# A two-layer decoder trunk on one core: gate columns moved into the value projection, feed-forward loads two units ahead, linear-attention outputs grouped by rows, first loads reordered, half of the compression copies on GpSimd

## The chip, the cores and the metric

The kernel runs on one core of a Trainium2 chip. The metric is the device time of one execution in microseconds (us), the median over runs. The core has five engines with an instruction queue each: TensorE (PE, matmuls), VectorE (DVE), ScalarE (ACT), GpSimd (POOL) and SyncE (SP, which only issues DMA transfers). An engine runs its queue in order; an instruction that waits for another engine or a transfer holds up all that stand behind it.

## What is computed

A trunk of two layers on x of 1024 tokens by 1024 channels, in fp32. The first mixes with gated linear attention and with cross-attention to a memory of 256 tokens; the second with native sparse attention (NSA) and the same kind of memory attention. Each is followed by a convolutional feed-forward network.

```
# layer A
q, k, v, r, alr, mq = split_cols(h @ w_in, [GLA_QK, GLA_QK, GLA_V, GLA_V, GLA_RANK, MEM_WIDTH])
...
# linear attention, chunk by chunk, with the state S
o_inter = jnp.einsum('bthd,bhde->bhte', qc * jnp.exp(b), S)
o = o_inter + jnp.einsum('bhts,bhse->bhte', attn, vc)
...
# after layer A, once: six key and value tensors
kv = (rmsnorm(x, g_kv) @ w_kv).reshape(B, T, 6, NSA_GROUPS, NSA_DH)
k_c, v_c, k_s, v_s, k_w, v_w = [kv[:, :, i] for i in range(6)]
...
# compressed blocks: 16 + 16 tokens each, plus a position term, through a small MLP
blocks = jnp.concatenate([sub[:, i:i + ncmp] for i in range(n_sub)], axis=2)
blocks = blocks + pe[:, None, :]
```

Layer B projects the normalised x to 512 NSA queries, 24 branch gates (three for each of eight heads, through a sigmoid) and 512 memory queries.

## The kernel before

The tokens are worked in two halves of 512. A tile holds 128 channels (or 128 tokens) on the partitions. A value that goes through PE at full precision is split in a high part (ACT, fp32r) and a low part (DVE, the difference), and a projection is three matmuls per 128 channels: high by high, high by low, low by high (`projg`, lines 192 to 194). `wraw` loads 128x1024 weights over SP, `wsplit` splits them (lines 176 and 177). The names with r and l at their end (wqkr, wqkl) are such parts. The program records all instructions first and a scheduler orders them on each engine by their dependences; `follow` pins one instruction behind another, and `weave` and `blend` interleave two streams of work by given weights. Buffers are rings: `U` 14 tiles of 128x512, `V` 32 of 128x1024, raw weights 4, split weights 6.

The start (`mix_a`, `stats`, `qkv_a`): x comes in eight tiles over SP, the first weights behind the first of them, the constants over ACT and POOL. ACT squares x for the norm, splits the weights and makes the high parts h (line 227), DVE the low parts (line 228); then four qk projections follow, the results scaled by the norm afterwards.

Linear attention (`gla`): a chunk's outputs go are, for each of four heads, a matmul from the state (line 835: 64 rows, since two heads share a tile) and one from the masked products A with the values (line 842: 128 rows). Both are plain fp32, which PE runs as a pair of instructions each. The four heads are done one after another; the first chunk has no state.

Feed-forward (`Up`, `run`): 22 units, each with two raw tiles wu (four loads over SP), splits into A, Ah and Al (ACT line 978, DVE line 979), sums of weight columns on POOL, and matmuls into fx, fy and fw (lines 1014 to 1016). The raw tiles and the split tiles have rings of two units. `run` works one unit and prepares the next: it issues the next unit's loads at its own beginning.

Before layer B (`mix_b`): for each half and for kind 0 and 1 (compressed keys and values), `front` projects to kc, scales it by the norm rs to kcs (DVE line 1450), and `comp_in` copies it into the block layout ck: eight copies per kind and half, on ACT (lines 1458 and 1459), with a step of 16 elements in the source. When both halves are in, DVE adds the position term pe (line 1465), and the matmuls hid read ck. `front` then projects the gates from a packed 24-column weight (`packed`, lines 219 and 220: a 128x512 matmul for 24 columns in use) to gsb, which matmuls gateT (line 1549) turn to token rows: ope. `MemKV(1)` projects the memory's keys mk meanwhile, from the split weights wmkr and wmkl. `values` projects the sparse attention's values nv: 256 columns for each 128 tokens (lines 1618 to 1620), with the weights wnv scaled by the norm's gain on DVE or POOL.

## Time and profile before

| | us |
|---|---|
| median of three runs | 2321.58 |
| lowest and highest | 2311.52, 2324.42 |
| the profiled execution | 2315.45 |
| its span | 2313.7 |
| PE busy | 2256.4 (98%) |
| DVE busy | 1735.4 (75%) |
| ACT busy | 1139.0 (49%) |
| POOL busy | 365.4 (16%) |

The profile is of one execution. The span runs from its first to its last instruction. A share of busy time is a mean over stages that differ; what an engine waits for is in the views of waits and the timeline, and the clock that TensorE was granted is in the windows: 1.00 is 2.4 GHz, and there are two levels, 2.4 and 1.2 GHz.

### The profile page before, as it was taken

The numbers are of one execution on the slowest core, as the hardware profiler recorded it, in microseconds if no ns is written. First come the engines' busy times: TensorE is split into PE (matmuls) and PEld (weight loads), VectorE is DVE, ScalarE is ACT, GpSimd is POOL, SyncE is SP. The second block draws the span as 40 slices with busy tenths as digits, with TensorE's granted clock in tenths as the row PEclk, the third lists the DMA queues.
The fourth block names the chain that finished last, engine by engine and source line by source line (L and its number), as shares of the span: only waits on it lengthen the run. The fifth ranks groups of instructions, "written<-read, shape, count | busy, mean of one in ns | idle before, by whom it ended". The sixth has DMA issues, their size and how long they took to land.

```text
span 2313.7 us, 31260 instructions
## 1 busy us (share of the span) xinstructions
PE 2256.4 (98%) x11062; PEld 1839.1 (79%) x11062; DVE 1735.4 (75%) x3086; ACT 1139.0 (49%) x2081; POOL 365.4 (16%) x333
## 2 busy tenths in 40 slices
PE   8999999999999999999999999999999999999998
PEld 6888777877788888888888877767887888888886
DVE  6785776887876768886656688885888777667877
ACT  5463544543333334456544588774543343334445
POOL 1211310004322210000002121110003422210000
PEclk9999999999999999999999999999999999999999
DMA  6333236433433329543421111007434433228533
GB/s 212 101 108 95 64 130 210 139 112 135 137 105 113 100 81 340 176 132 125 128 74 53 41 39 45 8 22 240 148 129 137 141 105 110 96 83 323 183 98 110
DMA packets 138893, 284.96 MB, mean 123 GB/s; under 512 B 16086, under 2 KB 22403, under 8 KB 138736
## 3 DMA queue, kind: packets, MB, share of 16 engines
q1 hardware_dynamic: 130144, 262.20, 34.7%
q0 software_dynamic: 3840, 12.24, 1.6%
q10 hardware_dynamic: 4752, 8.51, 1.0%
q8 instruction: 87, 1.43, 0.3%
q14 instruction: 70, 0.57, 0.1%
HBM read 211.06 MB, written 71.83 MB: 122 GB/s over the span
## 4 chain that ended last, share of the span: by engine, by line
PE 84%; DVE 7%; DMA 4%; ACT 3%; issue 2%; SPq 1%; POOL 0%; DVEq 0%; ACTq 0%; POOLq 0%
PE dn L1342 5%; PE dn L1341 5%; PE dn L1343 5%; PE fy L1014 5%; PE fy L1016 4%; PE fy L1015 4%; PE fx L1014 3%; PE no L1753 3%; PE fx L1015 3%; PE fx L1016 3%; PE fw L1016 3%; PE fw L1015 3%; PE fw L1014 3%; PE npt L1737 2%; PE op L193 2%; PE op L192 2%
## 5 line engine op out<-in xcount | busy, mean ns | idle before, releaser
L1342 PE MATMUL dn<-db,da 128*128 128x512 f32 (+1 forms) x628 | 242.4, 386 | 0.8 <-DVE db L1271 0.6
L1341 PE MATMUL dn<-db,da 128*128 128x512 f32 (+1 forms) x628 | 242.5, 386 | 0.0
L1343 PE MATMUL dn<-db,da 128*128 128x512 f32 (+1 forms) x628 | 241.7, 385 | 0.0
L1014 PE MATMUL fy<-B,Ah 128*128 128x512 f32 x496 | 195.1, 393 | 11.3 <-DVE q L1048 6.6
L1016 PE MATMUL fy<-B,Al 128*128 128x512 f32 x496 | 193.6, 390 | 0.4 <-DVE Al L979 0.4
L1015 PE MATMUL fy<-B,Ah 128*128 128x512 f32 x496 | 193.5, 390 | 0.0
L978 ACT ACTIVATE Ah<-wu 128x1024 fp32r<-128x1024 f32 x124 | 130.4, 1052 | 100.9 <-PE fy L1015 60.3
L998 POOL TENSOR_TENSOR wu<-wu,wu 128x512 f32<-128x512 f32 x36 | 49.3, 1369 | 744.4 <-DVE Al L979 410.6
L979 DVE TENSOR_TENSOR Al<-wu,Ah 128x1024 fp32r<-128x1024 f32 x124 | 158.0, 1275 | 6.6 <-ACT Ah L978 6.6
L1342 PEld LDWEIGHTS dn<-db,da 128*128 128x128 f32 x628 | 117.9, 188 | 26.4 <-DVE db L1271 2.6
L1016 PE MATMUL fw<-B,Al 128*128 128x512 f32 x352 | 137.8, 391 | 0.0
L1341 PEld LDWEIGHTS dn<-db,da 128*128 128x128 f32 x628 | 118.0, 188 | 24.3 <-issue 0.2
L1015 PE MATMUL fw<-B,Ah 128*128 128x512 f32 x352 | 137.1, 389 | 0.0
L1014 PE MATMUL fw<-B,Ah 128*128 128x512 f32 x352 | 137.0, 389 | 0.0
L1343 PEld LDWEIGHTS dn<-db,da 128*128 128x128 f32 x628 | 117.9, 188 | 23.3
L1271 DVE TENSOR_TENSOR db<-bl,db 128x512 fp32r<-128x512 f32 x154 | 105.6, 686 | 27.2 <-ACT db L1270 26.6
L1014 PEld LDWEIGHTS fy<-B,Ah 128*128 128x128 f32 x496 | 93.4, 188 | 36.3 <-DVE q L1048 10.4
L1270 ACT ACTIVATE db<-bl 128x512 fp32r<-128x512 f32 x154 | 95.7, 621 | 30.2 <-PE dn L1343 20.8
L1016 PEld LDWEIGHTS fy<-B,Al 128*128 128x128 f32 x496 | 93.4, 188 | 20.7 <-DVE Al L979 1.1
L1015 PEld LDWEIGHTS fy<-B,Ah 128*128 128x128 f32 x496 | 93.4, 188 | 18.9
L192 PE MATMUL op<-om,wor 128*128 128x512 f32 x256 | 103.1, 404 | 2.2 <-ACT om L224 2.2
L1270 ACT ACTIVATE da<-wb 128x512 fp32r<-128x512 f32 x88 | 55.0, 629 | 101.9 <-PE dn L1342 64.6
(427 smaller groups left out, 6176.4 us busy)
## 6 DMA issues: line engine op xcount, KB each, us to landing
wu<-in_w_up_dram SPq DMA_DIRECT2D x176, 256.0 KB, 3.1
bl<-gb_d SPq DMA_DIRECT2D x154, 256.0 KB, 2.7
gb_d<-fc SPq DMA_DIRECT2D x132, 256.0 KB, 3.0
wb<-in_w_down_dram SPq DMA_DIRECT2D x44, 256.0 KB, 4.5
wa<-in_w_down_dram SPq DMA_DIRECT2D x22, 512.0 KB, 7.8
wo<-in_a_wo_dram SPq DMA_DIRECT2D x16, 512.0 KB, 3.7
xre<-om_d SPq DMA_DIRECT2D x32, 256.0 KB, 4.7
x_r<-x SPq DMA_DIRECT2D x32, 256.0 KB, 2.6
```

What stands on the lines that cost most here:

```text
L192: mm(ps, wr[:, k, :], hr, start=(k == 0), stop=False)
L978: a = nc.scalar.activation(hi, src, AF.Copy)
L979: b = nc.vector.tensor_tensor(lo, src, f(hi), ALU.subtract)
L1014: mm(ps, wr, hr, start=(first and j == 0), stop=False, skip_group_check=True)
L1015: mm(ps, wr, hl, start=False, stop=False, skip_group_check=True)
L1016: mm(ps, wl, hr, start=False, stop=(stop and j == 3), skip_group_check=True)
L1270: nc.scalar.activation(w[:, hs(0)], t, AF.Copy)
L1271: b = tt(w[:, hs(1)], t, f(w)[:, hs(0)], ALU.subtract)
L1341: mm(o, hi, bh, start=first, stop=False, skip_group_check=True)
L1342: mm(o, hi, bl, start=False, stop=False, skip_group_check=True)
L1343: mm(o, lo, bh, start=False, stop=stop or n == NP - 1, skip_group_check=True)
L1753: mm(acc[a * 64 : a * 64 + 64, :256], v, pf[:, a * 256 : (a + 1) * 256], start=(n == 0), stop=(n == last[a]),)
```

## The change

Five edits.

1. First loads. The first weights come in two halves, each behind one of the first two tiles of x; the gains that h needs come as a small tile cg of their own over ACT's queue; the other constants (cs, idu, wal, mskf) go over SP behind the second weights. ACT makes all h before any square (the squares are pinned behind, `Norm.past`); a projection's result is scaled once rs is there. Fourteen 128x128 fp32 matmuls on a constant tile are put at PE's beginning.

2. Linear attention: the matmuls of a chunk are ordered by their rows, 128-row ones of two heads, then the four from the state, then the other two of 128 rows.

3. Feed-forward: `run` gets the unit after next, and issues its loads (`ahead`) behind the split of the third and fifth parts.

4. Compression: of each pair of copies the second goes to POOL.

5. Gates: the 24 gate columns stand behind the 256 value columns, so nv has 280 columns, token rows already; `values` scales both parts by their gains, and makes ope from the last 24 columns. The packed weight, its projection, gsb, fold and gateT go.

```diff
+    warm = PS("warm")
+    for _ in range(14):
+        mm(warm[:, :P], on_d, on_d, start=True, stop=True)
...
             for k2 in range(4):
                 t = V(s="x0")
                 tv = t.rearrange("p (k t) -> p k t", k=2)
                 if half == 0:
                     for i in range(2):
-                        last_x[0] = nc.sync.dma_start(tv[:, i, :], x[2 * k2 + i, :, hs(half)])
-                        if k2 + i == 0:
-                            w0.append(wraw(a_w[2], s="wqk"))
+                        nc.sync.dma_start(tv[:, i, :], x[2 * k2 + i, :, hs(half)])
+                        if k2 == 0:
+                            nc.sync.dma_start(raw[:, hs(i)], a_w[2, :, hs(i)])
...
-                        h.append(rl(tv[:, i, :], col(C_MIX + 2 * k2 + i), s="h"))
-                        if k2 + i == 0:
-                            w0[0] = wsplit(w0[0], s="wqk")
+                        k = 2 * k2 + i
+                        t = V(F32R, "h")
+                        h.append((t[:, :HT], t[:, HT:]))
+                        if k2 == 0:
+                            rl_into(wr[:, hs(i)], wl[:, hs(i)], raw[:, hs(i)])
+                        n.past = rl_into(*h[-1], tv[:, i, :], cg[:, k : k + 1])
...
-                    if len(late) > 1:
+                    if len(late) > 1 and rs[half] is not None:
                         evac(*late.pop(0))
...
-        drain(take(st, 16))
-        follow(nc.gpsimd.dma_start(idu, kst[:, : 2 * P]), last_x[0], "order")
-        follow(nc.gpsimd.dma_start(wal, w_alpha), last_x[0], "order")
+        drain(take(st, 8))
+        qa = qkv_a(0, h[0], nc.sync)
+        drain(take(qa, 5))
         mf = U(s="mskf")
-        follow(nc.gpsimd.dma_start(mf[:, :448], msk), last_x[0], "order")
+        for to, src in ((cs, cst), (idu, kst[:, : 2 * P]), (wal, w_alpha), (mf[:, :448], msk)):
+            nc.sync.dma_start(to, src)
...
+                    inner(0, True, first)
+                    if not first:
+                        decayed(0, False)
+                        decayed(1, True)
+                    inner(1, first, True)
...
+        def ahead(then, after):
+            if after is not None:
+                after.load()
+            if then is not None and then.early:
+                then.again()
+
+        def run(u, last, then, after):
             nxt = [then] if then is not None else []
-            each(nxt, "load")
-            if u.early:
-                u.again()
-            elif u.s1 is None:
+            if u.s1 is None:
                 u.p1()
...
                 u.split35((then.kept, u.opened))
+                ahead(then, after)
                 u.p7()
...
                     nc.scalar.activation(ck[0:64, :, g, 32 * half : 32 * half + 32], pv[gr, js, :], AF.Copy)
-                    nc.scalar.activation(
-                        ck[64:128, :, g, 32 * half - 1 + m0 : 32 * half + 31], pv[gr, js, m0:], AF.Copy
-                    )
+                    nc.gpsimd.tensor_copy(ck[64:128, :, g, 32 * half - 1 + m0 : 32 * half + 31], pv[gr, js, m0:])
...
-            pg = PS("gate")
-            packed_proj(pg, wg, h[half])
-            t = U(s="gsb")
-            nc.vector.tensor_tensor(t[0:64, :], pg[0:64, :], rs[half][0:64, :], ALU.mult)
-            gsb.append(t)
-            yield 3.6
...
+            NG = 256 + 24
...
+                for c0, c1, gain in ((0, 256, G_KV), (256, NG, G_B)):
+                    part = rv[:, :, c0:c1]
+                    g = cs[:, gain + 2 * k2 : gain + 2 * k2 + 2].unsqueeze(2).broadcast_to([P, 2, c1 - c0])
+                    eng.tensor_tensor(part, part, g, ALU.mult)
...
-                        o = ps[:, :256]
+                        o = ps[:, :NG]
...
+                tok = rst[half][:, c : c + 1]
+                nc.scalar.activation(val[half][:, c * 256 : (c + 1) * 256], ps[:, :256], AF.Copy, scale=tok)
+                nc.vector.tensor_scalar(ope[:, 4 * half + c, :], ps[:, 256:NG], tok, -87.0, ALU.mult, ALU.max)
                 yield 0.1
+            og = ope[:, 4 * half + cs_[0] : 4 * half + cs_[-1] + 1, :]
+            nc.scalar.activation(og, og, AF.Exp, scale=-1.0)
+            nc.vector.tensor_scalar(og, og, 1.0, None, ALU.add)
```

What the scheduler makes of it shows at three places. The rows are an engine's instructions in the order in which they stand in its queue: line, operation, output<-inputs.

On PE, the outputs of the second chunk of the linear attention; before:

```order
552 L835 MATMUL go_1163<-qe_1135,state_1261 128x128
553 L842 MATMUL go_1163<-A_550,vt_544 128x128
554 L835 MATMUL go_1163<-qe_1135,state_1261 128x128
555 L842 MATMUL go_1163<-A_550,vt_544 128x128
556 L835 MATMUL go_1164<-qe_1135,state_1261 128x128
557 L842 MATMUL go_1164<-A_550,vt_544 128x128
558 L835 MATMUL go_1164<-qe_1135,state_1261 128x128
559 L842 MATMUL go_1164<-A_550,vt_544 128x128
```

and now:

```order
555 L857 MATMUL go_1183<-A_570,vt_564 128x128
556 L857 MATMUL go_1184<-A_570,vt_564 128x128
557 L846 MATMUL go_1183<-qe_1155,state_1281 128x128
558 L846 MATMUL go_1184<-qe_1155,state_1281 128x128
559 L846 MATMUL go_1183<-qe_1155,state_1281 128x128
560 L846 MATMUL go_1184<-qe_1155,state_1281 128x128
561 L857 MATMUL go_1183<-A_570,vt_564 128x128
562 L857 MATMUL go_1184<-A_570,vt_564 128x128
```

The 128-row matmuls (A by vt) and the 64-row ones (state by qe) no longer alternate.

On DVE, behind the kcs of kind 0 in the second half (ck by pe are the position additions, wmkl the low parts of the memory-key weights, macc the sums of squares of the memory); before:

```order
1211 L1450 TENSOR_TENSOR kcs_8472<-kc_8447,rs_8398 128x512
1212 L1465 TENSOR_TENSOR ck_8253<-ck_8253,pe_8251 128x1024
1213 L1465 TENSOR_TENSOR ck_8254<-ck_8254,pe_8251 128x1024
1214 L177 TENSOR_TENSOR wmkl_8611<-wmk_8608,wmkr_8610 128x1024
1215 L1450 TENSOR_TENSOR kcs_8509<-kc_8484,rs_8398 128x512
1216 L1465 TENSOR_TENSOR ck_8255<-ck_8255,pe_8251 128x1024
1217 L1479 TENSOR_TENSOR gsb_8538<-gate_8521,rs_8398 64x512
1218 L1465 TENSOR_TENSOR ck_8256<-ck_8256,pe_8251 128x1024
1219 L344 TENSOR_TENSOR macc_8540<-mem_8421 128x256
1220 L177 TENSOR_TENSOR wmkl_8642<-wmk_8639,wmkr_8641 128x1024
```

and now:

```order
1207 L1475 TENSOR_TENSOR kcs_8466<-kc_8441,rs_8382 128x512
1208 L177 TENSOR_TENSOR wmkl_8584<-wmk_8581,wmkr_8583 128x1024
1209 L1488 TENSOR_TENSOR ck_8273<-ck_8273,pe_8271 128x1024
1210 L1488 TENSOR_TENSOR ck_8274<-ck_8274,pe_8271 128x1024
1211 L1475 TENSOR_TENSOR kcs_8503<-kc_8478,rs_8382 128x512
1212 L348 TENSOR_TENSOR macc_8515<-mem_8415 128x256
1213 L177 TENSOR_TENSOR wmkl_8615<-wmk_8612,wmkr_8614 128x1024
1214 L1488 TENSOR_TENSOR ck_8275<-ck_8275,pe_8271 128x1024
1215 L1488 TENSOR_TENSOR ck_8276<-ck_8276,pe_8271 128x1024
1216 L350 TENSOR_TENSOR macc_8515<-macc_8515,mem_8415 128x256
1217 L177 TENSOR_TENSOR wmkl_8657<-wmk_8654,wmkr_8656 128x1024
```

The third wmkl (8642, now 8615) stands two rows behind the last addition of pe before, and ahead of the last two now.

On DVE at the third feed-forward unit (A, Al are low parts, wu the raw weights, q reads the matmul result fy); before:

```order
526 L1000 TENSOR_TENSOR wu_3505<-wu_3506,wu_3505 128x512
527 L1001 TENSOR_TENSOR wu_3506<-wu_3506,wu_3505 128x512
528 L979 TENSOR_TENSOR A_3518<-wu_3507,A_3518 128x512
529 L1048 TENSOR_TENSOR q_4062<-fy_4049,s_719_4047 128x512
530 L979 TENSOR_TENSOR Al_3811<-wu_3508,Ah_3810 128x1024
```

and now:

```order
525 L999 TENSOR_TENSOR Al_3829<-wu_3527,Ah_3828 128x1024
526 L1021 TENSOR_TENSOR wu_3526<-wu_3526,wu_3525 128x512
527 L1068 TENSOR_TENSOR q_4082<-fy_4069,s_721_4067 128x512
528 L999 TENSOR_TENSOR Al_3831<-wu_3528,Ah_3830 128x1024
529 L999 TENSOR_TENSOR A_3538<-wu_3527,A_3538 128x512
```

The part A, which waited at the head of these three, stands at their end.

## Rows read from the trace of the kernel before

**Rows 1.** The page: the span, and busy time, share and instructions of each engine.

```profile
span 2313.7 us, 31260 instructions
...
PE 2256.4 (98%) x11062; PEld 1839.1 (79%) x11062; DVE 1735.4 (75%) x3086; ACT 1139.0 (49%) x2081; POOL 365.4 (16%) x333
```

**Rows 2.** Waits of PE: line, releaser, us in total, times, longest.

```profile
PE qk L192 <- ACT h L227: 9.4, 1, 9.4
PE fy L1014 <- DVE q L1048: 6.6, 7, 1.4
```

**Rows 3.** Windows: us; busy of PE, PEld, DVE, ACT, POOL; clock; DMA share; GB/s.

```profile
4.00:10.00 6.00, 0.62 (x1) 0.29 (x1) 2.48 (x3) 4.12 (x7) 0.34 (x1) 1.00 1.02 370
19.00:23.00 4.00, 3.75 (x10) 2.97 (x10) 3.16 (x5) 0.06 (x1) 0.00 (x0) 0.57 0.50 158
514.00:518.00 4.00, 4.00 (x12) 3.13 (x12) 4.00 (x8) 0.63 (x1) 0.00 (x0) 0.57 0.25 69
1121.00:1129.00 8.00, 4.71 (x22) 4.72 (x23) 7.33 (x11) 2.51 (x3) 0.00 (x0) 0.57 0.44 142
```

**Rows 4.** Timeline of the start: start, duration, engine, line, operation, count, [idle before<-releaser].

```profile
5.79 1.06 ACT L176 ACTIVATE wqkr<-wqk 128x1024 fp32r<-128x1024 f32 x1 [0.71 <-DMA wqk<-in_a_w_dram]
...
9.36 5.70 DVE L228 SCALAR_TENSOR_TENSOR h<-x,cs,h 128x512 fp32r<-128x512 f32 x8
...
17.22 0.50 PE L192 MATMUL qk<-h,wqkr 128*128 128x512 f32 x1 [0.38 <-ACT wqkr L176]
...
19.25 0.57 PE L194 MATMUL qk<-h,wqkl 128*128 128x512 f32 x1 [1.29 <-DVE wqkl L177]
```

**Rows 5.** Timeline of PE at outputs go of the first chunks.

```profile
138.87 1.05 PE L842 MATMUL go<-A,vt 128*128 128x128 f32 x8
...
150.36 0.48 PE L835 MATMUL go<-qe,state 64*128 64x128 f32 x2
150.78 0.49 PE L842 MATMUL go<-A,vt 128*128 128x128 f32 x2
...
181.72 0.49 PE L835 MATMUL go<-qe,state 64*128 64x128 f32 x4
182.14 0.71 PE L842 MATMUL go<-A,vt 128*128 128x128 f32 x4
```

**Rows 6.** Timeline of the feed-forward stage at its third unit.

```profile
503.34 0.69 DVE L979 TENSOR_TENSOR A<-wu,A 128x512 fp32r<-128x512 f32 x1 [0.64 <-ACT A L978]
...
504.55 1.22 DVE L979 TENSOR_TENSOR Al<-wu,Ah 128x1024 fp32r<-128x1024 f32 x1
...
510.63 1.06 ACT L978 ACTIVATE Ah<-wu 128x1024 fp32r<-128x1024 f32 x1 [2.77 <-DMA wu<-in_w_up_dram]
...
513.72 0.50 PE L1014 MATMUL fy<-B,Ah 128*128 128x512 f32 x1 [2.72 <-ACT Ah L978]
```

**Rows 7.** Instructions that touch ck: durations in ns (min, median, max), first and last start.

```profile
L1458 ACT ACTIVATE ck<-kcs x16: 627/640/663, 1087.1 to 1120.2; 64x256 f32<-64x256 f32 x16
```

**Rows 8.** Groups of POOL: line, operation, shapes, count, busy us, mean ns, idle before.

```profile
L760 POOL TENSOR_TENSOR z<-dec,gq 64x512 f32<-64x512 f32 x14 | 32.4, 2316 | 130.5 <-ACT dec L750 130.4
...
L1510 POOL CAST kl<-kl 64x512 fp32r<-64x512 f32 x8 | 4.9, 610 | 0.5
```

**Rows 9.** Timeline at the memory-key projection of layer B.

```profile
1121.54 1.22 DVE L1465 TENSOR_TENSOR ck<-ck,pe 128x1024 f32<-128x1024 f32 x1 [0.81 <-ACT ck L1459]
...
1123.01 1.22 DVE L177 TENSOR_TENSOR wmkl<-wmk,wmkr 128x1024 fp32r<-128x1024 f32 x1
...
1124.29 0.58 PE L194 MATMUL mk<-mh,wmkl 128*128 128x256 f32 x1 [4.99 <-DVE wmkl L177]
```

**Rows 10.** Windows of one tile's instructions alone: gate, then nv; PE's busy time first.

```profile
1091.40:1095.06 3.66, 3.63 (x16) 2.81 (x15) 0.00 (x0) 1.00 0.00 0
...
1278.60:1290.10 11.50, 11.46 (x96) 11.46 (x96) 0.83 (x3) 1.00 0.43 119
```

**Rows 11.** Timeline of PE at the first of the matmuls gateT.

```profile
1252.57 1.51 PE L1549 MATMUL gateT<-fold,gsb 64*128 64x24 f32 x12
```

More of the change, by code (lines that the diff above doesn't have):

```diff
@@ L199, in proj, with packed @@
         drain(projg(ps, w, h))
-    def packed(src, n, s, gain=None, after=None):
+    def packed(src, n, s, gain=None, eng=None):
         raw = S([P, 256], s="praw", bufs=1)[:, : KT * n]
-        d = nc.gpsimd.dma_start(raw, src)
-        if after is not None:
-            follow(d, after, "order")
+        (eng or nc.gpsimd).dma_start(raw, src)
         if gain is not None:
@@ L251, in __init__ @@
             self.w = width
+            self.past = None
         def square(self, xt, s):
             t = U(s=s)[:, : self.w]
-            nc.scalar.activation(t, xt, AF.Square)
+            a = nc.scalar.activation(t, xt, AF.Square)
+            if self.past is not None:
+                follow(a, self.past, "order")
             return t
@@ L644, in second_x, with qkv_a @@
                 yield 1.0
-        def qkv_a(half, h, after=None):
+        def qkv_a(half, h, eng=None):
             kt, qt = V(s="gk"), V(s="gq")
@@ L661, in qkv_a @@
                     late.append((ps, q, hp))
-                    if len(late) > 1:
+                    if len(late) > 1 and rs[half] is not None:
                         evac(*late.pop(0))
-            evac(*late.pop())
-            wq = packed(a_walr, 16, "walr", after=after)
+            while late:
+                evac(*late.pop(0))
+            wq = packed(a_walr, 16, "walr", eng=eng)
             pa = PS("alr")
@@ L1149, in run @@
                 u.split35((u.kept, u.opened))
+                ahead(then, after)
                 u.p7()
@@ L1184, in ffn @@
         then = order[0]
-        then.load()
+        each(order[:2], "load")
         each(pair, "p4")
@@ L1192, in ffn @@
         last = pair
-        for u, then in zip(order, order[1:]):
-            run(u, last, then)
+        for u, then, after_ in zip(order, order[1:], order[2:] + [None]):
+            run(u, last, then, after_)
             last = [u]
@@ L1475, in front @@
                 comp_in(kind, half, ps)
[L1476 to L1483 removed]
+        weave((front(0), 10.4), (second, 9.0))
         mkv = MemKV(1)
@@ L1544, in mix_b @@
         weave((mem_all(), 107.0), (compress(), 15.0))
-        pg = PS("gateT")
-        for qt in range(8):
-            t = gsb[qt // 4][0:64, (qt % 4) * P : (qt % 4 + 1) * P]
-            mm(pg[:, qt * 24 : (qt + 1) * 24], t, fold, start=True, stop=True)
-        opf = ope.rearrange("p a b -> p (a b)")
-        nc.vector.tensor_scalar(opf, pg[:, :192], -87.0, None, ALU.max)
-        nc.scalar.activation(opf, opf, AF.Exp, scale=-1.0)
-        nc.vector.tensor_scalar(opf, opf, 1.0, None, ALU.add)
         kcr = [S([P, 2, P], F32R, s="state", bufs=2) for _ in range(2)]
```

77 lines of the change are left out of this document (37 added, 40 removed).

## The prediction

> **What bounds the kernel now.** I read the page's busy times first: TensorE (PE) is busy 2256.4 us of a span of 2313.7 us [rows 1], so it idles 57.3 us in all, and no other engine is near it. The end can therefore move in three ways: less work on PE, less of its idle time, or less work done at half clock. The waits of PE say where the idle time is: 9.4 us before its first projection matmul, 6.6 us in seven pieces in the feed-forward stage [rows 2], and 5.0 us at one place before a memory-key (mk) matmul [rows 9]. The windows show the third kind: after such waits the granted clock of a stretch falls to a mean of 0.57, that is, most of it runs at 1.2 instead of 2.4 GHz [rows 3]; four such microseconds hold 4 x (1 - 0.57) = 1.7 us less work. The profiled execution took 2315.45 us, 1.75 us more than its span, and 6.1 us less than the median of 2321.58. I make the sum against the profiled execution. Half a per cent (11.6 us) is about what a measurement of this kernel can tell from no change.
>
> **1. First loads, early matmuls.** Before, the split of the first weights starts at 5.79 us when their load has landed, ScalarE (ACT) does squares before it comes to h, and PE starts at 9.4 us [rows 2, 4]. It is then paced by VectorE's (DVE) low parts of h: eight in 5.70 us, 0.71 us each [rows 4], while PE's three matmuls per part are 3 x 0.227 us (16 in 3.63 us, [rows 10]). The first projection leaves off at 17.22 - 0.38 = 16.84 us; the second waits 0.38 us for ACT and 1.29 us for DVE, which was adding squares meanwhile [rows 4], and the stretch behind that is at 0.57 [rows 3].
> After: ACT's order is the weights in two halves, eight h, the next weights, and only then squares; DVE's the same. Before the first h can start, x0, x1 and both halves must land, 1.05 MB; before, x0 and the weights (0.79 MB) were there at 5.79 us with the constants' loads competing, which now come later. I take 5.8 us; half a split 0.6, an h 0.7: PE at 7.1 us. DVE follows with eight parts of 0.71 us from there, 12.8 us, and two matmuls more: 13.3 us instead of 16.84, gain 3.5. The loads allow this: 2.6 MB at the 370 GB/s of [rows 3] are 7.1 us; begun at about 2.5 us (an estimate from the 0.79 MB at 5.79 us), the last x lands near 9.7 us, and DVE comes to it near 12. The second split is directly behind the last h on both engines; its load lands 0.5 MB later, near 11.1 us, so of the 1.67 us of stall some 0.2 stay: gain 1.4. The 14 small fp32 matmuls on PE have nothing to wait for but a memset; I take it that the clock is up when the first h comes and stays so, with the stalls gone, so the half-clock stretch of 1.7 us goes too. Sum **6.6 us**. Bounds: 2 (the second weights land late, the stall and the clock loss stay, and the early matmuls don't help) to 8 (PE starts at 6 us).
>
> **2. Outputs grouped by rows.** A chunk is 16 instructions (each fp32 matmul is a pair). Before, a 64-row pair and a 128-row pair alternate, 0.42 us per pair (150.36 to 150.78): eight pairs, 3.35 us. In the first chunk, with 128-row matmuls alone, eight instructions take 1.05 us up to the end of the last, 0.11 us apart; two 64-row pairs together take 0.42 us, 0.105 each [rows 5]. So only a switch between the shapes costs some 0.1 us per instruction. After: four of 128 rows, eight of 64, four of 128: 16 x 0.11 and two switches of 0.1, 1.95 us. That is 1.4 us less for a chunk. Seven chunks have both shapes; in two of them, by the order and as at 181.72, others or equals stood between already, so I count five: **7.0 us**. Some of it can turn into waits where DVE sets the pace. Bounds 2.3 (a rival below) and 9 (all seven by 1.3).
> The Trainium skill ("TensorE: Matmul & The Clock Gate", Part 3: packing small matmuls) has a rule against this: a weight load overlaps a running matmul only when the two are in different row groups. By it 128-row matmuls in a row could not overlap their loads at all, and the trace disagrees: they stand 0.11 us apart [rows 5].
>
> **3. Feed-forward loads two units ahead.** SP's order in the steady part of the stage is the same before and after, load for load, since each load waits for its buffer and not for its place in the program; so the pieces of 1.4 us before fy, seven in all [rows 2], stay. Only the front changes: on DVE the low part Al, after which a load of wu can start, stood behind the A of 503.34 and a q; now it stands before that A. The A takes 0.69 us and waited 0.64 for ACT [rows 6], so the load starts some 1.2 us earlier and PE's wait of 2.72 us at 513.72 becomes 1.5. **1.2 us**; bounds 0 and 4.4 (the whole wait and the 1.7 us of half clock behind it [rows 3]).
>
> **4. Compression copies on GpSimd (POOL).** Before, ACT makes all 32, 0.64 us each, from 1087.1 us on [rows 7]. The mk matmul of 1124.29 waits for the DVE part wmkl of 1123.01, which stands in DVE's order behind the additions of pe, and the last of those waits for ACT's last copies at 1121.54 [rows 9]. After, 16 copies (10.2 us) leave ACT; the rs of the second half, which ACT reaches only behind the first 16 copies, comes earlier; and DVE has wmkl ahead of the second pair of additions. PE comes earlier too, by the gate matmuls (part 5). It came to the waiting matmul at 1124.29 - 4.99 = 1119.3, so in the same clock it now comes at 1112.0. Back from there, two mk projections (48 x 0.119), 16 hid matmuls (0.11 each, as in [rows 5]) and a kc projection (24 x 0.227) are 12.9 us: the first kc of that half ends at 1099.1. With p for one POOL copy, four copies, two additions (1.22 each, the first beside the copies) and the rest of DVE's order, wmkl is there at 1103 + 4p. Next late would be the sum of squares of the memory, wanted at 1114.7: behind four more copies, an addition, a wmkl and six sums of 0.42 it is there at 1106.7 + 8p. So nothing waits up to p = 1.0 us, and 1.3 us at 1.16. The trace has no such copy on POOL (64 rows, 256 elements with steps of 64 bytes). Nearest are a cast of 64x512 at 0.61 us and a product of 64x512 with two strided inputs at 2.32 us [rows 8]: for 256 elements 0.3 to 1.16. I take 0.65 (one input as in the cast, steps as in the product). The wait of 4.99 us goes, and the 22 matmuls behind it run at 0.119 us (96 in 11.46 us, [rows 10]) instead of 4.71 / 22 = 0.214 [rows 3]: 2.1 us. **7.1 us**; bounds 5.8 (1.16) and 7.1 by this, 2.5 if half the wait stays and the clock falls all the same.
> The Trainium skill ("GPSIMD Engine Reference", section 7: performance pitfalls) puts a read with steps over 8 bytes at about 2.9 cycles per element, which with its 1.2 GHz (section 1) would be some 0.6 us for 256, an estimate from that page; no row here shows such a copy.
>
> **5. Gate columns in the value projection.** Removed on PE: 32 gate matmuls, 0.227 us each [rows 10], 7.3 us; 16 gateT instructions, 12 of them in 1.51 us [rows 11], 1.9 us. Added: 192 nv matmuls of 280 instead of 256 columns, 24 x 0.119 / 256 = 0.011 us each, 2.1 us. **7.1 us** less, in stages where PE hardly waits. The small new operations (24-column gains, eight ope products, three exponentials) lie on DVE, ACT and POOL beside the nv matmuls; for waits they bring I take off 0.5 us, bounds 0 and 3.
>
> **Sum**: 6.6 + 7.0 + 1.2 + 7.1 + 7.1 - 0.5 = 28.5 us. Against the profiled execution that is 2287.0, against the median 2293.1; the next median can lie at either, so I say 2290.
>
> **Rivals.**
> *GpSimd is the new bound* (the other side). POOL's 16 copies run one after the other from 1087.1 on, so for a long p the sum of squares is there at 1087 + 16p + 5 and PE waits 16p - 22.7. The whole sum of 28.5 us is eaten at p = 3.2; at p = 4 PE waits 41.3 us and the time is 2315.45 - 28.5 + 41.3 = 2328. For it: POOL's strided product takes 2.32 us. Against: that is for 512 elements and two inputs [rows 8].
> *The start is bound by its loads.* x arrives no faster, the second weights land after 13 us, the stall comes again with its clock. Part 1 is 2: 2294.6. For it: SP's queue holds the later x loads until earlier ones have landed.
> *Loads of weights don't overlap inside one row group*: then after the change inner pairs stay at 0.205 and only the change between the two 64-row halves overlaps; a chunk is 8 x 0.205 + 8 x 0.155 = 2.9 us, part 2 is 5 x 0.45 = 2.3: 2294.7. Against: [rows 5]. It is the skill's rule cited above.
> *The gains don't arrive.* The chain goes on through DVE, whose work is not less; if PE is earlier but DVE is what is waited for in the second linear-attention half and in the sparse stage, half of parts 2 and 5 are given back, and with part 1 or 4 failing too some 12 us are left: 2309.
>
> **Numbers.** Forecast, with all large terms within a few us: 0.58 (2281 to 2298). Start bound by its loads: 0.14; no overlap within a row group: 0.08 (2294 to 2302, together at its end). Gains not arriving: 0.14 (2302 to 2316). GpSimd as bound: 0.06 (2310 to 2330). The range 2277 to 2307 leaves out the upper part of the last two and a little below. Faster needs less than 2310: 0.87; same 0.09; slower 0.04.
>
> **What would show it.** Right: PE's first projection matmul near 7 us and the second projection without a stall of over 0.5 us; go instructions 0.11 us apart within a group; no wait of PE before mk, and POOL copies under 1 us; no gate rows, nv matmuls about 0.011 us further apart; the fy waits still there. Wrong: copies of over 1.3 us with DVE's additions waiting for POOL; a clock of 0.57 still behind the start; new waits of PE for DVE or ACT in the sparse stage that add to more than 3 us.

## The result

| | before | changed |
|---|---|---|
| median, us | 2316.81 | 2291.78 |
| lowest and highest | 2311.52, 2324.42 | 2287.47, 2292.84 |
| executions | 6 | 6 |
| span of the profiled execution | 2313.7 | 2290.5 |

The changed kernel takes 0.9887 of the time, with an interval of 0.9866 to 0.9909: about 25 us less. The prediction was 2290, from a sum of 28.5 us; the spans of the two profiles differ by 23.2 us. The total is right, but not every term of it: the first edit, forecast at 6.6 us, brought about 2 us by itself, and a remedy for loads that it made late brings 3.5 to 6 us more.

### The profile page after: what moved, and what is told of

It reads as the page before. It is cut to its first block, busy times and chain, and to the rows that moved or that the text cites. A ratio compares the mean times of both kernels' runs of the same rounds, so it can differ in the third digit from the quotient of the medians.

```text
span 2290.5 us, 31253 instructions
## 1 busy us (share of the span) xinstructions
PE 2244.0 (98%) x11042; PEld 1831.0 (80%) x11042; DVE 1738.3 (76%) x3095; ACT 1128.7 (49%) x2067; POOL 376.0 (16%) x351
## 4 chain that ended last, share of the span: by engine, by line
PE 83%; DVE 8%; DMA 3%; ACT 3%; issue 2%; POOL 0%; SPq 0%; DVEq 0%; ACTq 0%; POOLq 0%
PE dn L1367 6%; PE dn L1368 6%; PE dn L1366 6%; PE fy L1034 5%; PE fy L1036 4%; PE fy L1035 4%; PE fx L1034 3%; PE no L1768 3%; PE fx L1035 3%; PE fx L1036 3%; PE fw L1036 3%; PE fw L1035 3%; PE fw L1034 3%; PE op L195 2%; PE op L196 2%; PE op L194 2%
## 5 line engine op out<-in xcount | busy, mean ns | idle before, releaser
L1296 DVE TENSOR_TENSOR db<-bl,db 128x512 fp32r<-128x512 f32 x154 | 105.5, 685 | 28.5 <-ACT db L1295 27.9
```

What stands on the lines that cost most here:

```text
L1296: b = tt(w[:, hs(1)], t, f(w)[:, hs(0)], ALU.subtract)
```

## The profile after

The page of the changed kernel: the span, and busy time of each engine.

```profile
span 2290.5 us, 31253 instructions
...
PE 2244.0 (98%) x11042; PEld 1831.0 (80%) x11042; DVE 1738.3 (76%) x3095; ACT 1128.7 (49%) x2067; POOL 376.0 (16%) x351
```

PE is still the bound, with 12.4 us less work than in [rows 1] and 10.8 us less idle time (46.5 instead of 57.3). The waits of PE (us in total, times, longest) say which idle time is left:

```profile
PE gv L695 <- DVE gk L666: 1.7, 1, 1.7
PE mms L356 <- DVE macc L350: 1.5, 1, 1.5
...
PE qk L194 <- ACT h L227: 1.3, 1, 1.3
```

The 9.4 us at the start of [rows 2] are 1.3, and the 5.0 us before mk of [rows 9] are gone, with a wait of 1.5 before mms in their place. New is gv, the first value projection of layer A, which waits for gk. (The waits of fy for q, 6.6 us in [rows 2], are 4.0 us in five pieces here.) The windows (busy of PE, PEld, DVE, ACT, POOL; clock; DMA share; GB/s) answer to [rows 3]; the matmuls of its third and fourth stretch now lie about 8 and 22 us earlier:

```profile
4.00:10.00 6.00, 4.38 (x25) 3.51 (x25) 3.86 (x6) 4.46 (x8) 0.00 (x0) 1.00 1.03 349
19.00:23.00 4.00, 4.00 (x20) 3.30 (x19) 3.15 (x5) 1.92 (x3) 1.46 (x2) 1.00 0.48 136
...
505.00:511.00 6.00, 5.77 (x26) 4.44 (x25) 6.00 (x10) 1.53 (x3) 0.00 (x0) 1.00 0.29 85
1085.00:1105.00 20.00, 20.00 (x131) 18.25 (x129) 14.33 (x20) 15.19 (x25) 10.47 (x12) 1.00 0.23 79
```

The clock is 1.00 in all of them. The timeline of the start answers to [rows 4]: PE's first and second projection, and DVE's eight low parts of h.

```profile
7.45 5.39 DVE L228 SCALAR_TENSOR_TENSOR h<-x,cg,h 128x512 fp32r<-128x512 f32 x8
7.47 0.50 PE L194 MATMUL qk<-h,wqkr 128*128 128x512 f32 x1 [1.33 <-ACT h L227]
...
13.68 0.47 PE L194 MATMUL qk<-h,wqkr 128*128 128x512 f32 x1
...
14.90 0.50 PE L196 MATMUL qk<-h,wqkl 128*128 128x512 f32 x1 [0.52 <-DVE wqkl L177]
```

The second projection starts at 13.68 instead of 17.22 us, with a stall of 0.5 instead of 1.7 us. The second chunk's outputs on PE, against [rows 5]:

```profile
149.32 0.61 PE L857 MATMUL go<-A,vt 128*128 128x128 f32 x4
149.85 0.71 PE L846 MATMUL go<-qe,state 64*128 64x128 f32 x8
150.50 0.71 PE L857 MATMUL go<-A,vt 128*128 128x128 f32 x4
150.97 0.36 PE L435 MATMUL msc<-mK,mq 128*128 128x256 f32 x1
```

From its first start to that of msc the chunk takes 150.97 - 149.32 = 1.65 us, where eight pairs of 0.42 were 3.35. This is the second chunk; the four of the second half look the same, one of them at half clock. The third takes 2.55 us, since its two kinds alternate once more, and the fourth's matmuls stand apart between other work. The copies into ck (ns: min, median, max), against [rows 7]:

```profile
L1483 ACT ACTIVATE ck<-kcs x16: 620/656/667, 1078.3 to 1098.9; 64x256 f32<-64x256 f32 x16
L1484 POOL COPY ck<-kcs x16: 605/622/1697, 1078.4 to 1101.0; 64x248 f32<-64x248 f32 x8, 64x256 f32<-64x256 f32 x8
```

And the first 96 nv matmuls of 280 columns, as a window of that tile alone, against the second of [rows 10]:

```profile
1255.10:1267.60 12.50, 12.46 (x96) 12.27 (x96) 0.43 (x2) 1.09 (x3) 1.00 0.40 118
```

12.46 instead of 11.46 us for 96: 0.010 us for each.

**Where the 23.2 us come from.** Starts on PE of the same matmul in four profiles, in us. "Again" is a second profile of the changed kernel, and the last kernel is the changed one with one group of loads moved (both experiment 3); the differences are to before:

| matmul | before | changed | difference | again | difference | loads moved | difference |
|---|---|---|---|---|---|---|---|
| alr, the first | 38.67 | 32.69 | -6.0 | 32.39 | -6.3 | 32.12 | -6.6 |
| z, the first | 65.87 | 61.87 | -4.0 | 64.00 | -1.9 | 59.30 | -6.6 |
| msc | 153.52 | 150.97 | -2.6 | 150.08 | -3.4 | 145.38 | -8.1 |
| mo, second half | 340.32 | 335.04 | -5.3 | 328.89 | -11.4 | 323.61 | -16.7 |
| ms, feed-forward's begin | 391.81 | 384.32 | -7.5 | 377.02 | -14.8 | 371.82 | -20.0 |
| ms, layer B's begin | 1070.59 | 1061.03 | -9.6 | 1052.46 | -18.1 | 1045.71 | -24.9 |
| mms | 1129.02 | 1106.58 | -22.4 | 1098.18 | -30.8 | 1091.35 | -37.7 |
| kcmp (from praw and state) | 1256.17 | 1232.63 | -23.5 | 1225.27 | -30.9 | 1216.89 | -39.3 |
| span | 2313.7 | 2290.5 | -23.2 | 2285.4 | -28.3 | 2276.2 | -37.5 |

The start gains 6.0 to 6.3 us by alr, and 2.0 and 4.4 us of that are gone by z in the two profiles of the changed kernel. Copies and gates give 13.9 us between 1070.59 and 1256.17, and 12.8 in the second profile.

Start and linear attention together give 7.5 us in the first profile and 14.8 in the second, where the terms said 6.6 + 7.0: the same kernel, 7.3 us apart. From z to the feed-forward's begin the first is 9.4 us slower. Four stretches at half clock that only the first has there (from 76, 97, 281 and 308 us on, 1.7 us each) are 6.8 us of it, and a wait of 2.1 us before an msc, for ACT's mq, is most of the rest. So what is missing behind z in the first profile belongs to that execution; what both profiles lose is lost between alr and z.

## Experiments

Three theories on the missing part. **A**: a load of the start that stands later in its queue makes PE wait, so that the start's gain is given back there. **B**: in linear attention DVE is what is waited for, and POOL's products z slow it, so that earlier matmuls only wait longer. **C**: the stretches at half clock have moved, and take back what was won. Ratios are to the kernel before on the same chip.

### 1. Each edit alone

Edit 1, first loads and early matmuls, on the kernel before:

```diff
+    for _ in range(14):
+        mm(warm[:, :P], on_d, on_d, start=True, stop=True)
...
+        for to, src in ((cs, cst), (idu, kst[:, : 2 * P]), (wal, w_alpha), (mf[:, :448], msk)):
+            nc.sync.dma_start(to, src)
```

> The kernel before with the first edit alone (first loads, early matmuls). Theory 1, the terms of the prediction add: the whole 6.6 us reach the end, 6 to 7 us faster than before. Theory 2, the linear attention's second half is paced by VectorE (busy in all of 250 to 282 us of both traces), and what is won ahead of it does not pass it: the first projection matmul at 7.5 us as in the changed kernel, but the first levels matmuls of that stretch at most 2 us earlier, the outputs behind it (the first go after 300 us) within 1 us of before, and the time within 2 us of before.

Measured: 2309.09 us against 2312.42, ratio 0.9993 (0.9981 to 1.0005). Its first projection matmul stands at 7.72 us and its first alr at 32.18 us, 6.5 us earlier than before, and yet the end hardly moves. Among its waits of PE up to 110 us:

```profile
PE gv L696 <- DVE gk L667: 2.9, 1, 2.9
```

The wait before gv is there without any of the other edits, so edit 1 brings it; no row of before has it. The first z is only 1.9 us earlier than before, and behind the wait the clock falls:

```profile
38.00:46.00 8.00, 5.15 (x17) 4.13 (x17) 7.53 (x14) 5.82 (x12) 0.00 (x0) 0.79 0.42 132
50.00:110.00 60.00, 57.51 (x323) 50.56 (x322) 45.06 (x59) 29.53 (x42) 11.13 (x7) 0.94 0.33 104
```

The wait of 2.9 and 8 x 0.21 = 1.7 us of lost clock are the 4.6 us between alr and z. From 50 to 110 us another 60 x 0.06 = 3.6 us go to the clock, which is 1.00 there in the profile of before: with that the rest is gone in this execution, which was the longest of its ten. By the ratio the edit is worth 0.0007 x 2312.42 = 1.6 us (from 1.2 slower to 4.4 faster), so 6.6 lies outside. The loss begins at gv, long before the stretch that theory 2 names.

Edit 2, outputs grouped by rows:

```diff
+                    inner(0, True, first)
+                    if not first:
+                        decayed(0, False)
+                        decayed(1, True)
+                    inner(1, first, True)
```

> The kernel before with the second edit alone (outputs grouped by rows). Theory 1: 7 us faster, 1.4 us at each of five chunks. Theory 2: the chunks ahead of the stretch from 250 to 282 us give nothing at the end, those behind it do: 3 to 5 us faster.

Measured: 2304.58 us, ratio 0.997 (0.9956 to 0.9983): 0.003 x 2312.42 = 6.9 us (3.9 to 10.2), the predicted 7.0. Of theory 2's 3 to 5 us the interval holds only the upper part.

Edit 4, half of the copies on POOL:

```diff
-                    nc.scalar.activation(
-                        ck[64:128, :, g, 32 * half - 1 + m0 : 32 * half + 31], pv[gr, js, m0:], AF.Copy
-                    )
+                    nc.gpsimd.tensor_copy(ck[64:128, :, g, 32 * half - 1 + m0 : 32 * half + 31], pv[gr, js, m0:])
```

> The kernel before with the fourth edit alone (half of the compression copies on GpSimd, gate matmuls still there). Theory 1: the wait of 4.99 us before the memory keys and the 2.1 us at half clock behind it go, 7 us faster, and nothing waits for the sum of squares of the memory, since TensorE comes later by the gate matmuls. The rival, in which the gain came from the gates: less than 2 us.

Measured: 2305.98 us, ratio 0.9977 (0.9961 to 0.9994): 5.3 us (1.4 to 9.0). PE has no wait at all between 1060 and 1180 us, and the window in which mk stands runs at full clock:

```profile
1115.00:1135.00 20.00, 20.00 (x140) 18.67 (x139) 16.03 (x24) 8.10 (x11) 0.00 (x0) 1.00 0.61 206
```

Edit 5, gate columns in the value projection:

```diff
-            pg = PS("gate")
-            packed_proj(pg, wg, h[half])
...
+            NG = 256 + 24
```

> The kernel before with the fifth edit alone (gate columns in the value projection, all copies still on ScalarE). Theory 1, the terms add: 7.1 us faster. The rival, in which the gate matmuls lay in front of a wait for ScalarE and covered it: their 7.3 us turn into a longer wait before the memory keys (12 us in place of 5), and the whole is within 2 us of before.

Measured: 2310.98 us, ratio 0.9994 (0.9982 to 1.0006): 1.4 us (at most 4.2), which can't be told from none, though 7 us of PE's work are gone. Its waits of PE from 1060 to 1180 us, and two windows:

```profile
PE mms L351 <- DVE macc L345: 4.7, 1, 4.7
PE hid L1516 <- DVE ck L1464: 2.5, 1, 2.5
```

```profile
1105.00:1115.00 10.00, 8.02 (x53) 7.99 (x54) 6.59 (x7) 8.78 (x13) 0.00 (x0) 0.83 0.28 77
1115.00:1135.00 20.00, 15.31 (x83) 14.00 (x82) 14.54 (x21) 9.04 (x13) 0.00 (x0) 0.83 0.52 167
```

PE comes earlier to hid and to mms, whose inputs hang on ACT's copies, and waits 7.2 us in place of 5.0; the clock has a mean of 0.83 for 30 us, where before it has it for the last 20 of them. That is 2.2 us more of waits and 10 x 0.17 = 1.7 us more of lost clock, over half of the 7.1: without edit 4, much of edit 5's gain is lost there.

Edits 4 and 5 together:

> The kernel before with the fourth and the fifth edit together. Alone they gave 0.23% (5.3 us) and 0.06% (1.4 us). Theory 1 (the gate matmuls covered a stretch in which ScalarE's copies set the pace; each edit takes away what the other needs): together 12 to 14 us, more than the 6.7 of the sum. Rival (they add): 6 to 8 us.

Measured: 2300.82 us against 2313.95, ratio 0.9952 (0.9935 to 0.9969): 11.1 us (7.2 to 15.0), where the two alone add to 6.7. The intervals are too wide to show by the times alone that the pair is worth more than its parts. Of the waits of over half a microsecond between 1060 and 1180 us one is left, 1.5 us at mms for macc.

Edit 3, loads two units ahead:

```diff
                 u.split35((then.kept, u.opened))
+                ahead(then, after)
                 u.p7()
```

> The kernel before with the third edit alone (feed-forward loads two units ahead). Theory 1: only the front of the stage changes; the wait of 2.72 us before the fy matmul of the third unit becomes 1.3 to 1.5 us, some microseconds more or less with the half-clock stretch behind it, and the five or so waits of about 1.4 us before later fy matmuls are still there: 1 to 3 us faster at most. Rival (the loads really come two units ahead): those later waits go too, 5 us and more faster.

Measured: 2313.82 us against 2311.76, ratio 1.0007 (0.9994 to 1.002): no gain that can be told, and none excluded: the interval goes from 1.4 us faster to 4.6 us slower. The waits of PE in the first feed-forward stage, 390 to 880 us:

```profile
PE fw L1015 <- DVE B L225: 2.0, 1, 2.0
PE fy L1014 <- ACT Ah L978: 1.3, 2, 0.9
```

The wait for Ah fell, from 3.6 us in this stretch of before to 1.3 (its longest was the 2.72 of [rows 6]); but a wait of 2.0 us before an fw matmul, for B, is new. The other traces agree: in this stretch PE waits for Ah 2.0 to 3.9 us in the six without this edit and 1.1 to 1.4 us in the eight with it, and B brings 0.5 to 2.0 us in seven of these eight and nothing in any of the six. On the mean some 1.9 us go and 0.9 come: what is left is about a microsecond, too little for these runs to tell.

### 2. The early matmuls

The changed kernel without them:

```diff
-    for _ in range(14):
-        mm(warm[:, :P], on_d, on_d, start=True, stop=True)
```

> The changed kernel without the 14 early matmuls on a constant tile. Theory 1 (they have the clock up when the first projection comes): without them the first projection runs at 1.2 GHz for some microseconds, its matmuls 0.43 us apart, and TensorE is 1.5 to 2 us later at the end of the qk projections (the first low-rank gate matmul alr at about 34.5 us in place of 32.7). Rival (the pace is that of VectorE's h anyway, and the clock rises at once): alr within 0.5 us of 32.7.

Measured: 2299.52 us against 2313.95, ratio 0.9944 (0.9926 to 0.9963); the changed kernel has 0.9887, and 0.9898 when it ran again (experiment 3). The first h, and PE's first matmul, come at 8.85 us. Further on in PE's timeline:

```profile
14.49 0.63 PE L190 MATMUL qk<-h,wqkr 128*128 128x512 f32 x1
14.92 0.46 PE L191 MATMUL qk<-h,wqkr 128*128 128x512 f32 x1
15.22 0.40 PE L192 MATMUL qk<-h,wqkl 128*128 128x512 f32 x1
15.46 0.39 PE L190 MATMUL qk<-h,wqkr 128*128 128x512 f32 x1
```

From its third matmul up to 14.92 us the projection's matmuls start 0.43 us apart, and from 15.46 on 0.23, as in the changed kernel from its third matmul on. So behind an idle PE the first 6 us go at half the pace, and behind the 28 instructions on a constant they do not. (The clock column reads 1.00 in both; that it is the lower level is argued from the distances alone.) At its first sums ms and at its first alr (35.61 us, where theory 1 said 34.5) this kernel is 2.9 us behind the changed one. Of these 1.4 us are its first h, which came at 8.85 in place of 7.47 us; so the pace is worth about 1.5, as theory 1 had it. The ratios differ by more, 10.6 to 13.2 us. Its profiled execution was the shortest of its five, 2292.23, and doesn't show the rest, which stays open.

### 3. The memory's loads (theory A)

What stands before the four mem loads in SP's order: before three wv loads, now all four (rows of SP's program, before and then changed):

```
10 L159 DMA wqk_325<-in_a_w_dram 128x1024
11 L159 DMA wv_400<-in_a_wv_dram 128x1024
12 L159 DMA wv_454<-in_a_wv_dram 128x1024
13 L159 DMA wv_484<-in_a_wv_dram 128x1024
14 L326 DMA mem_246<-in_mem_dram 128x512
...
16 L205 DMA praw_378<-in_a_walr_dram 128x128
17 L161 DMA wv_414<-in_a_wv_dram 128x1024
18 L161 DMA wv_450<-in_a_wv_dram 128x1024
19 L161 DMA wv_504<-in_a_wv_dram 128x1024
20 L161 DMA wv_534<-in_a_wv_dram 128x1024
21 L330 DMA mem_297<-in_mem_dram 128x512
```

The raw weights have a ring of four, so the fourth wv waits until the first is split, and that waits for the end of the second qk projection. The timeline of the changed kernel:

```profile
25.43 1.23 DVE L177 TENSOR_TENSOR wvl<-wv,wvr 128x1024 fp32r<-128x1024 f32 x1 [3.25 <-PE qk L195]
...
27.12 2.47 SPq L330 DMA_DIRECT2D mem<-in_mem_dram  x4
...
29.98 0.69 DVE L245 TENSOR_TENSOR rs<-rs,rt 128x512 f32<-128x512 f32 x1
...
34.63 3.31 ACT L227 ACTIVATE mh<-mem,cs 128x256 fp32r<-128x256 f32 x8 [5.78 <-DMA mem<-in_mem_dram]
...
39.48 1.28 DVE L666 SCALAR_TENSOR_TENSOR gk<-qk,rs 128x512 f32<-128x512 f32 x2
...
40.22 0.50 PE L695 MATMUL gv<-wvr,h 128*128 128x512 f32 x1 [1.71 <-DVE gk L666]
```

Before, SP issued mem from 22.48 us on, ACT began mh at 29.43 and DVE gk at 34.51. Now the loads go out 4.6 us later; ACT stands with mh at its head, idle for 5.8 us, DVE for ACT behind it, and gk, behind mh on DVE, starts 5.0 us later than before although PE's projections are 6 us earlier. The norm rs, gk's other input, was ready at 30.7. The remedy puts these four loads in POOL's queue:

```diff
-        mkv.load(nc.sync)
+        mkv.load(nc.gpsimd)
```

> The changed kernel with the four loads of the memory tokens on GpSimd's queue in place of SyncE's. Theory 1: the wait of 1.71 us before the value matmul gv at 40.2 us comes from these loads: they stand on SyncE's queue behind the moved constants and the wv loads, issue at 27.1 us (before: 22.5), and VectorE's low parts of the memory, which wait for them, stand in its queue ahead of the gk that frees a PSUM buffer. Then the wait goes, TensorE is 1.7 to 2 us earlier at the first z matmul (60 us in place of 61.9). Rival: gk is late because rs is (rs is ready at 30.6 us in both); then the wait stays within 0.5 us.

Measured: 2280.61 us against 2313.95, ratio 0.9872 (0.985 to 0.9895). To tell a few us, it ran again, on the same chip as the changed kernel again:

> The changed kernel again, beside the next one on one chip: 0.987 to 0.990 of the time before. In a second profile the waits should be those of the first, while the stretches at half clock may lie elsewhere.

> The changed kernel with the memory's loads on GpSimd's queue again, in more rounds. Theory 1 (the late memory loads cost the wait before gv and, through it, the steady clock in the linear attention): 4 to 10 us faster than the changed kernel on the same chip, 0.983 to 0.986 of the time before. Rival (its first profile was a lucky one, and only the wait of 1.7 us goes): within 3 us of the changed kernel.

Measured: the changed kernel 2287.23 (2284.24 to 2293.09), ratio 0.9898 (0.9881 to 0.9914); with the loads moved 2281.51 (2278.06 to 2288.05), ratio 0.9872 (0.9853 to 0.9892). That is 5.7 us less by the medians, within theory 1's 4 to 10, though the ratio is above its 0.983 to 0.986. By the ratios it is 6.0 us less here and, from the first runs of both kernels (0.9872 and 0.9887), 3.5. Both pairs of intervals overlap a little, so the size isn't settled. The timeline of the second run:

```profile
22.42 2.12 POOL L330 DMA_DIRECT2D mem<-in_mem_dram  x4
28.20 3.44 ACT L227 ACTIVATE mh<-mem,cs 128x256 fp32r<-128x256 f32 x8
35.15 1.29 DVE L666 SCALAR_TENSOR_TENSOR gk<-qk,rs 128x512 f32<-128x512 f32 x2
35.75 0.39 PE L695 MATMUL gv<-wvr,h 128*128 128x512 f32 x1
```

gv starts at 35.75 instead of 40.22 us without a wait, and the whole 6.6 us are still there at the first z. The first run with the loads moved has z at 59.19 us too. The changed kernel's second profile, for comparison, has a longer wait before gv than its first, and the clock falls behind it:

```profile
PE gv L695 <- DVE gk L666: 2.5, 1, 2.5
...
40.00:45.00 5.00, 4.27 (x12) 3.37 (x13) 5.00 (x9) 3.55 (x7) 0.00 (x0) 0.66 0.40 125
```

2.5 + 5 x 0.34 = 4.2 us; with the loads moved z is 4.7 us earlier than there, and of the 5.2 us between these two profiles at the feed-forward's begin nearly all are there at z. So theory A holds for the start. That the wait also costs the steady clock in the linear attention, as theory 1 had it, isn't shown: this second profile has the wait, and the clock reads 1.00 from 60 to 400 us. This version has the lowest medians of the study.

### 4. Who sets the pace in linear attention (theory B)

The changed kernel with all products z on DVE:

```diff
-                    (nc.vector, nc.gpsimd)[p].tensor_tensor(zv, d5, q5, ALU.mult)
+                    nc.vector.tensor_tensor(zv, d5, q5, ALU.mult)
```

> The changed kernel with the products z of the linear attention all on VectorE (GpSimd has half of them, 64 rows each). In the stretch from 250 to 310 us VectorE is busy throughout; instructions of one shape on it take 0.68 us or 1.7 to 2.5 us, the long ones while GpSimd's product runs. Theory 1 (the two engines hold each other up, and the stretch is paced by that): 14 products of 0.68 us more on VectorE, but no long ones; the stretch becomes shorter by 3 us or more. Rival (VectorE's load is what counts): the stretch is some 5 us longer, and the time 5 us slower than the changed kernel.

Measured: 2291.77 us against 2313.95, ratio 0.9913 (0.9895 to 0.9931): not faster than the changed kernel's 0.9887 and 0.9898; the intervals overlap, so the rival's 5 us slower isn't shown either. The window from 248 to 310 us of this kernel, and then of the changed one:

```profile
248.00:310.00 62.00, 57.16 (x314) 49.00 (x312) 59.68 (x90) 33.70 (x50) 1.90 (x2) 0.94 0.21 66
```

```profile
248.00:310.00 62.00, 54.58 (x301) 46.82 (x300) 60.21 (x81) 31.08 (x46) 19.82 (x12) 0.96 0.21 63
```

The long instructions on DVE are gone, as theory 1 had it. Of one shape, in the changed kernel and then in this one (ns: min, median, max):

```profile
L768 DVE TENSOR_TENSOR dec<-dec,gk x14: 666/690/1780, 87.6 to 290.6; 128x512 f32<-128x512 f32 x14
L768 DVE TENSOR_TENSOR dec<-dec,gk x14: 673/682/695, 86.2 to 288.6; 128x512 f32<-128x512 f32 x14
```

DVE is busy for about 60 of 62 us in both. Without POOL it does nine instructions more in the same busy time, and PE thirteen more, which fits; but the work taken over and new waits elsewhere (kdT for kd 3.4 us, gr for wrl 3.2) eat what that gives. DVE has hardly any idle time in this stretch; taking POOL away is no remedy, and B's size stays open.

### 5. How much POOL can take

All 32 copies on POOL:

```diff
-                    nc.scalar.activation(ck[0:64, :, g, 32 * half : 32 * half + 32], pv[gr, js, :], AF.Copy)
+                    nc.gpsimd.tensor_copy(ck[0:64, :, g, 32 * half : 32 * half + 32], pv[gr, js, :])
```

> The changed kernel with all 32 compression copies on GpSimd. In the changed kernel TensorE waits 1.5 us for the sum of squares of the memory, and VectorE's last two additions wait 0.5 and 1.2 us for GpSimd's copies (1.18 us each there, 0.62 alone). Theory 1 (GpSimd is now what is waited for): four more copies per kind and half, 16 in the second half, put its last copy back by 4 to 8 us; TensorE's wait there grows to 6 to 10 us and the kernel is 5 to 10 us slower than the changed one. Rival (the wait is VectorE's own load): ScalarE's relief makes up for it, the wait stays under 3 us.

Measured: 2296.01 us, ratio 0.9936 (0.9921 to 0.9952), 8.8 us above the changed kernel on the same chip. The copies have medians of 0.68 and 0.61 us, up to 1.7, and PE waits for what hangs on them:

```profile
PE mms L356 <- DVE macc L350: 7.5, 1, 7.5
```

So GpSimd can become the bound, at mms, as the rival of the prediction had it. Sixteen copies are already past the point where nothing waits: PE waits 1.5 us there.

## Why the prediction was right, and where it was not

**Right as worked out.** Part 2: a chunk at 1.65 us (predicted 1.95), and 6.9 us alone for 7.0. In that there is some luck: the trace of before has six chunks with alternating matmuls and not five, and with edit 2 alone five of them gain 1.7 us each (not 1.4) and the sixth 0.8. PE's busy time in the outputs falls by 8.1 us there, from 24.3 to 16.3. So the count and the gain of a chunk were both too low, and 7.0 is nearer than its terms. The rule of the Trainium skill ("TensorE: Matmul & The Clock Gate", Part 3) that weight loads don't overlap a matmul in the same row group is not what these rows show: the four 128-row matmuls from 149.32 on take 0.53 us up to the next group, 0.13 each, the eight of 64 rows 0.08 each, where alternating ones took 0.21 each. The rival by that rule had 2.9 us for the chunk. Part 5: an nv matmul longer by 0.010 us (0.011), the gates gone. Part 4: the wait before mk and the half clock behind it gone, a copy at 0.62 us where DVE left POOL alone (0.65). In this the trace agrees with the estimate of some 0.6 us that the prediction made from the Trainium skill ("GPSIMD Engine Reference", section 7). Beside DVE's work it was more, in the changed kernel's timeline:

```profile
1096.89 4.74 POOL L1484 COPY ck<-kcs 64x256 f32<-64x256 f32 x4 [2.88 <-DVE kcs L1475]
...
1101.66 1.23 DVE L1488 TENSOR_TENSOR ck<-ck,pe 128x1024 f32<-128x1024 f32 x1 [1.19 <-POOL ck L1484]
```

These four copies took 1.19 us each, DVE's last addition waited for them, and the sum of squares behind those was late by 1.5 us. The chain is the one that the prediction traced for its "next late", and one of its signs of being wrong came true there: single copies took up to 1.7 us, with DVE's additions waiting for POOL. Its line "nothing waits up to p = 1.0 us, and 1.3 us at 1.16" is for eight equal copies; these eight took 3.56 and 4.74 us for four each, a mean of 1.04, for which it gives 0.3 us. With the 1.19 of the last four it gives 1.5. So the place was right, the 0.65 too low for it, and the line counts the first four as much as the last four, which decide.

**Right, and probably not additive.** I costed parts 4 and 5 one by one, at 7.1 each. Alone they measured 5.3, with 7.1 inside its interval, and 1.4, with 7.1 outside; together 11.1. In the changed kernel's profile they give 13.9 us up to kcmp, where 7.1 + 7.3 + 1.9 were due; nv's longer matmuls come behind that. The prediction let PE come earlier by the gates when it traced part 4, so it had the pair right; it should have said that part 5's 7.1 are to be had only behind part 4. This rests on the waits that edit 5 brings alone and the pair does not, more than on the times.

**Wrong: part 1's 6.6 us carried to the end.** The places near the start were right: PE at 7.47 (7.1), the second projection at 13.68 (13.3), a stall of 0.5 (0.2), full clock, 6.0 us by alr. Alone it measured 1.6 us (at most 4.4), below the lower bound of 2. The bounds of part 1 were made from the first two projections only. The step that failed is the one that counted what SP's loads are moved past: I followed the constants, the weights and x, not the mem loads, which now stand behind a wv load that waits for its buffer. That took 2.0 and 4.4 of the 6 us back by z in the two profiles of the changed kernel, and by the remedy it is 3.5 to 6 us at the end. My rival "the start is bound by its loads" looked for the late load at 13 us; it came at 27 to 34. What that rival said for itself was also misread: before, the x loads of the start go out about 0.5 us apart (seven in 3.81 us from 1.64 us on), and it is the weight loads behind them that waited for x to land, 2.6 us in three pieces.

**Not decided: part 3.** 1.2 us were forecast; the interval, from 1.4 us faster to 4.6 slower, holds that, and it holds no gain at all too. The wait at that unit shrank, as worked out; that B would be late next, by 0.5 to 2.0 us in seven of eight traces, the prediction did not see.

**Open.** The singles by their ratios add to 0.7 + 3.0 + 2.3 + 0.6 - 0.7 = 5.9 thousandths, with edits 4 and 5 as a pair to 7.8, and the whole change gives 10.2 to 11.3. Part of the difference may be in the five intervals, part in edits that need each other. What the early matmuls do is open too: without them the changed kernel is 10.6 to 13.2 us slower by the ratios, while the whole of edit 1, alone, brought 1.6.

Theory C holds for single profiles: half-clock stretches explain most of the 9.4 us by which the two profiles of the changed kernel differ between z and the feed-forward's begin. No kernel here holds them in place, so what they are worth in the median isn't settled. From 10 to 400 us the mean clock is 0.99 in the profile of before, 0.98 in the first of the changed kernel, and 1.00 both in its second and in that of the last kernel. So the -14.8 and -20.0 us of these two at the feed-forward's begin are what the edits give where the clock takes next to nothing, and not what a median has; the last one's execution was also the shortest of its four.

## What to carry to other kernels

When loads are reordered, follow every later load on the same queue to the one that waits for a ring's buffer: the stall shows two stages on, at an engine that has another transfer's work at its head. Where PE waits for an engine, work taken off PE can turn into a longer wait, so cost edits around one wait as a pair, in both orders. A price for a copy read beside an idle engine is a lower bound where both engines are at work. And a difference of several us between two profiles can be the clock of one execution: take a second profile before explaining it.

## What the runs showed of the hardware

The places of the half-clock stretches differ between executions of one kernel. Windows of the changed kernel's first profile, and then of its second:

```profile
74.00:80.00 6.00, 6.00 (x40) 6.00 (x40) 3.17 (x7) 1.97 (x4) 0.00 (x0) 0.72 0.31 89
...
1099.00:1103.00 4.00, 4.00 (x36) 4.00 (x35) 2.56 (x3) 2.41 (x3) 2.53 (x3) 1.00 0.69 257
```

```profile
74.00:80.00 6.00, 6.00 (x52) 5.95 (x51) 3.45 (x6) 2.36 (x6) 0.00 (x0) 1.00 0.58 178
...
1099.00:1103.00 4.00, 4.00 (x22) 4.00 (x23) 3.24 (x6) 1.32 (x3) 0.00 (x0) 0.57 0.66 186
```

Work of the same stage runs at half clock in one and at full clock in the other. The matmuls of these windows lie some 2 us later and 8 us earlier in the second profile; there too, from 78 to 82 us in the second and from 1107 to 1111 in the first, the clock reads 1.00. A window of 4 us at 0.57 costs 4 x 0.43 = 1.7 us. In the first profile the clock fell at 76.3 us without a wait ahead of it, behind 16 matmuls of two columns:

```profile
73.03 1.93 PE L743 MATMUL diag<-ind,gqk 128*128 128x2 f32 x16
```

So a half-clock stretch in one profile need not be a property of the kernel. Of the two that the prediction priced, the one of the start, 1.7 us (19 to 23 us in before), is there in two of the six profiles of kernels with the same start, at 0.57 and 0.61, and reads 1.00 in four: it should have counted for a part. The one behind the wait of 5.0 us before mk, 2.1 us, is there in all four profiles that have this wait, at 0.50 to 0.58 in the 4 us behind it: that one came with its wait each time.

DVE and POOL are slower beside each other in this kernel: POOL's copies above by up to 1.19 / 0.62, and DVE's products by more. Products of one shape on DVE, in the changed kernel's timeline:

```profile
274.27 1.76 DVE L768 TENSOR_TENSOR dec<-dec,gk 128x512 f32<-128x512 f32 x1
...
277.89 0.67 DVE L768 TENSOR_TENSOR dec<-dec,gk 128x512 f32<-128x512 f32 x1
```

The first lies beside two products z on POOL (272.08 to 277.42 us), and takes 2.6 times as long as the next of the same shape. Without products on POOL (experiment 4) none of the 14 takes over 0.70 us.
